# Full-row score products, forget sums stored by heads, two spill buffers and an early first weight in a two-layer streaming encoder

## The chip, the core and the metric

One core of a Trainium2 chip runs the whole program in one launch. Its engines work side by side: TensorE (PE: products, with its weight loads listed apart as PEld), VectorE (DVE), ScalarE (ACT), GpSimd (POOL) and SyncE (SP), which issues the DMA transfers. Each engine takes its instructions in the order in which they were laid down at build time; an instruction that waits holds up all that stand behind it on its engine. The metric is the device time of one execution in microseconds (us).

## The reference

Two layers work on 1024 prompt rows and 32 sample rows of width 1024. Each has an input projection, two branches with gates, an output projection and a LayerNorm.

```
# layer 0
a = causal_dwconv(a_val * sigmoid(a_glu)); a = silu(LN(a)) * silu(a_gate)
ck = cumsum(log_sigmoid(f_logit + b_f))                    # per head
s = (q @ k.T) * 64**-0.5 + cq[:, None] - ck[None, :]       # 8 heads x 64, causal
o = softmax(s) @ v * silu(b_gate)
x = LN(alpha * x + concat(a, o) @ w_out)
# layer 1
c = multi_scale_pool(c_val) @ w_grp * scale * silu(c_gate)
score = sum_h iw[h] * relu(iq[h] @ ik.T / 8)               # 4 index heads x 64
keep the 256 best keys of each row; q, k, iq, ik are rotated (rope)
o = softmax(q @ k_kept.T * 64**-0.5) @ v_kept * silu(d_gate)
x = LN(alpha * x + concat(c, o) @ w_out)
```

Inputs and outputs are float32.

## The kernel before

**Numbers.** A float32 value is held as two fp32r tiles, a rounded high part and the rest (`split`: ACT rounds, DVE or POOL subtracts). A projection is three products, high weight by high input, low by high, high by low, 24 products for a group of 256 or 288 columns (`proj_steps`, L207). The low part of a 64-wide head is folded into the same 128 rows: `put_k` (L263) builds `kA` (rows 0 to 63 high part of the even head, rows 64 to 127 its low part) and `kB` (the odd head the other way round); `put_q` (L271) builds `q1` (the rounded pair of heads) and `qA`, `qB`, which hold the rest of q on the rows of the high part of k, and the rounded q on the rows of its low part.

**Score products.** `qk_mm` (L278) makes one tile of scores in two products into the same bank: L280 multiplies the 64 rows of one head of `q1` with 64 rows of `kA` or `kB`, and L281 multiplies all 128 rows of `qA` or `qB` with all 128 of the key tile. It is called in the attention of both layers (`first` in `attend`, 96 tiles each) and in the index scores of layer 1 (`scores`, 40 tiles).

**Attention.** `attend` goes over four pairs of heads p. In each, eight units (i, e), 256 queries of one head, are worked in a fixed order (`UNITS`). `merge` lays three streams side by side: `first` of a unit (score products, DVE adds bias and takes the running minimum at L362, ACT makes the exponential at L365), `second` of the unit before (PE transposes the exponentials at L411, ACT and DVE split them into `pth` and `ptl`, PE multiplies with v at L386), and the projections of the next pair's q and k (`qk0`, `qk1`), or, in the last pair, pieces of the output projection (`early_out`, L557). In layer 0 the bias of a tile is made by POOL (L891, L893) from `ckb`, a DMA of the head's running forget sums to all partitions (`fox_bias`, L887). The sums lie in the DRAM tile `ckd` by blocks of 128 keys, heads inside, so that one head is eight pieces of 512 bytes for every partition. When both heads of a unit are done, `spill` (L318) splits the result into `sph` and `spl`, one buffer each, and sends both to DRAM (`cod`); `cat_tiles` reads them back for the output projection.

**Start.** The nine row tiles of x come in (L671), PE transposes each (L252), ACT and DVE split them. The first weight is fetched and cut (`fetch`, `cut`) when the first projection asks for it; `start_plan` names the columns and `want` and `ready` run ahead by two.

**Between.** Layer 1 first projects index keys and queries (690 to 712 us), then v with the index scores in between (712 to 780), then finds the 256th best score of each row by halving intervals on DVE and ACT while the pooled mixer and the gates are projected (780 to 960), then builds the masks while the first q and k are projected.

**What sets the order.** The code is written in the order above; a scheduler at build time then places every instruction on its engine's queue. Tiles come from pools with a given number of buffers for each tag; a write to a buffer waits until the last reader of its former content is done. Tiles with the same tag share their buffers.

Of the kernel before, what the change touches and what calls it, by code (L numbers as in the profile page):

```python
# [10 lines left out]
FT = mybir.dt.float32  # L11
# [21 lines left out]
def tile_encoder(ctx: ExitStack, tc, A, O):  # L33
# [57 lines left out]
    ckd = dp.tile([11, 8, 128], FT, name="ckd")  # L91
# [10 lines left out]
    def split(hi, lo, src, eng=dve, alone=False):  # L102
        if alone:
            dve.tensor_copy(hi, src)
        else:
            act.activation(hi, src, AF.Copy)  # L106
        eng.tensor_tensor(lo, src, hi.bitcast(FT), op=OP.subtract)  # L107

    def fetch(src, c0, n, k0=0, kn=8):
        raw = wp.tile([128, 1056], FT, name="wraw", tag="wraw", bufs=2)  # L110
# [6 lines left out]
    def cut(raw, n, kn, own=None):  # L117
        if own is None:
            hi = wp.tile([128, 1056], FR, name="whi", tag="whi", bufs=3)
            lo = wp.tile([128, 1056], FR, name="wlo", tag="wlo", bufs=3)  # L120
# [124 lines left out]
    def to_xt(src, rows, X, t):  # L245
        g, off, _ = TT[t]
        for hf in range(2):
            ps = ps_t()
            pv = ps.rearrange("p (a n) -> p a n", a=4)
            for a in range(4):  # L250
                k = hf * 4 + a
                pe.transpose(pv[:, a, :rows], src[:rows, k * 128:(k + 1) * 128], ident[:rows, :rows])  # L252
            split(X[0][g][:, hf * 4:hf * 4 + 4, off:off + rows], X[1][g][:, hf * 4:hf * 4 + 4, off:off + rows],
                  pv[:, :, :rows])
# [16 lines left out]
    def put_q(q1, qA, qB, r):  # L271
        act.activation(q1, r, AF.Copy)  # L272
        act.activation(qA[64:128], r[0:64], AF.Copy)
        act.activation(qB[0:64], r[64:128], AF.Copy)
        dve.tensor_tensor(qA[0:64], r[0:64], q1[0:64].bitcast(FT), op=OP.subtract)
        dve.tensor_tensor(qB[64:128], r[64:128], q1[64:128].bitcast(FT), op=OP.subtract)
# [67 lines left out]
    def attend(l, ap, qk, stacks, bias_fn, last, order, early):  # L344


        def first(p, i, e, stacks, bias, pt):
            kA, kB, qs = stacks
            q1, qA, qB = qs[i]
            k2, q2 = (kA, kB)[e], (qA, qB)[e]  # L350
            for j in range(2):
# [6 lines left out]
                for c in range(nch):  # L358
                    c0, cn = c * 512, min(512, n - c * 512)
                    ps = ps_s()  # L360
                    qk_mm(ps[:, :cn], e, q1, q2, j * 128, 128, k2, c0, cn)
# [8 lines left out]
        def second(p, i, e, pt, v2, cat):  # L370
# [9 lines left out]
            def pv(pth, ptl, blocks):  # L380
# [10 lines left out]
                ot = ap.tile([128, 256], FT, name="ot", tag="ot", bufs=1)  # L391
                act.activation(ot[hb:hb + 64], po[64:128, :256], AF.Copy)
                dve.tensor_tensor(op[hb:hb + 64], po[0:64, :256], ot[hb:hb + 64], op=OP.add)
                if e == 1:
# [4 lines left out]
                    else:  # L399
                        spill(ap, cod[l][i][p], op)  # L400
# [256 lines left out]
    ckt = ep.tile([128, 11, 8], FT, name="ckt")  # L657
# [9 lines left out]
    with tc.tile_pool(name="p1", bufs=1, reuse_waits="tile") as p1:  # L667
        for t, (g, off, rows) in enumerate(TT):
            xt = p1.tile([128, D], FT, name="xrow", tag="xrow", bufs=3)
            src = A["x_prompt"][0, t * 128:(t + 1) * 128] if t < 8 else A["x_sample"][0]  # L670
            sp.dma_start(xt[:rows], src)  # L671
            to_xt(xt, rows, X0, t)
# [22 lines left out]
        start_plan(w0, [(c0 + c * 128, 128) for c in range(4) for c0 in (512, 0)])  # L695
# [31 lines left out]
        def wload_vf(k0, own=None):  # L727
            raw = wp.tile([128, 1056], FT, name="wraw", tag="wraw", bufs=2)
# [40 lines left out]
    def qk0(p):  # L769
# [6 lines left out]
        def evac(g, ps, nm, scale):  # L776
            if g % 2 == 0:
                hold[nm] = pz.tile([128, 544], FT, name=nm, tag=nm, bufs=1)
            r = hold[nm]
            c0 = 256 * (g % 2)  # L780
# [11 lines left out]
        def ev_q(g, t0, n, ps):  # L792
            r = evac(g, ps, "qr", SC)
            q1, qA, qB = (pz.tile([128, 256], FR, name=nm, tag=nm, bufs=4) for nm in ("q1", "qA", "qB"))
            c0 = 256 * (g % 2)
            put_q(q1, qA, qB, r[:, c0:c0 + 256])
            qs[g] = q1, qA, qB
            if n > 256:
                dve.tensor_copy(qkS0[:, p, 0, :], r[:, 512:544])
# [4 lines left out]
    def forget_sums():  # L804
# [3 lines left out]
        act.activation(ckt.rearrange("p t h -> p (t h)"), pck, AF.Copy)  # L808
# [33 lines left out]
    with tc.high_priority():  # L842
        rstd = p1r.tile([128, 1086], FT, name="rstd")
        for g, (s0, n) in enumerate(((0, 256), (256, 256), (512, 256), (768, 318))):
# [3 lines left out]
            pvv = ps_s()[:, :n]  # L848
            for c in range(4):
# [98 lines left out]
    masks = lp.tile([128, sum(MW)], BF, name="masks")  # L948
# [55 lines left out]
    with tc.tile_pool(name="p4", bufs=1, reuse_waits="tile") as p4:  # L1004
# [38 lines left out]
        for p in range(2):  # L1043
            q1, qA, qB = (p4.tile([128, SEQ - 256], FR, name=f"{nm}{p}") for nm in ("qi1", "qiA", "qiB"))
            qi_st.append((q1, qA, qB))

            def ev_iq(g, t0, n, ps, p=p, q1=q1, qA=qA, qB=qB):
# [535 lines left out]
```

## Time and profile before

| what | value |
|---|---|
| time, median of 3 executions | 1373.24 us (1371.05 to 1373.4) |
| time of the profiled execution | 1373.61 us |
| its span, first to last instruction | 1371.9 us |
| mean granted TensorE clock | 0.962 of 2.4 GHz |
| PE busy | 1290.8 us (94%) |
| DVE busy | 994.8 us (73%) |
| ACT busy | 694.1 us (51%) |
| POOL busy | 244.5 us (18%) |

The profile is of one execution; 1.7 us of its time lie outside the span. A busy share is an average over stages with different limits. PE counts as busy as long as any product is under way, and products overlap, so a busy PE can still lose time between the starts of its products; starts are therefore read one against the next. The clock of TensorE is granted at one of two levels, 2.4 GHz (shown as 1.00) or 1.2 GHz (0.50).

### The profile page before, as it was taken

How to read it: one execution, taken by the hardware profiler on the slowest of the kernel's cores; microseconds unless marked ns; L12 is line 12 of the kernel's file. 1: busy time of each engine (PE TensorE's matmuls, PEld its weight loads, DVE VectorE, ACT ScalarE, POOL GpSimd, SP SyncE). 2: the span in 40 equal slices, each digit the busy share in tenths (PEclk: the TensorE clock that was granted, in tenths of full speed). 3: DMA queues.
4: the chain of work that ended last, by engine and by line, in shares of the span. 5: the costliest groups of instructions: out<-in, count | busy, mean ns of one | idle time of the engine just before them, and what ended most of it. 6: DMA issues, size and time to landing. Idle time of an engine off the chain costs nothing. (4 is left out here: it accounts for less than half of the span.)

```text
span 1371.9 us, 25230 instructions
## 1 busy us (share of the span) xinstructions
PE 1290.8 (94%) x9341; PEld 1176.9 (86%) x9344; DVE 994.8 (73%) x2227; ACT 694.1 (51%) x1484; POOL 244.5 (18%) x529
## 2 busy tenths in 40 slices
PE   7999999999899998999999978699999999989997
PEld 6999999987787886899997778598988888868997
DVE  4699997374666666647846599995677878776467
ACT  4111232494766665512256676587356767675210
POOL 0000060003333332100021245365011000100000
PEclk9999999997999998999999998899999999999999
DMA  6113312333222356353242212123333223562502
GB/s 207 47 48 88 117 47 75 108 125 90 80 74 68 73 155 192 109 169 108 92 129 64 80 48 80 31 80 94 96 79 98 58 75 87 156 203 67 199 35 93
DMA packets 175063, 134.63 MB, mean 98 GB/s; under 512 B 37242, under 2 KB 163666, under 8 KB 174940
## 3 DMA queue, kind: packets, MB, share of 16 engines
q1 hardware_dynamic: 174940, 133.02, 33.3%
q8 instruction: 73, 1.20, 0.4%
q14 instruction: 50, 0.41, 0.1%
HBM read 85.09 MB, written 42.48 MB: 93 GB/s over the span
## 5 line engine op out<-in xcount | busy, mean ns | idle before, releaser
L841 DVE SCALAR_TENSOR_TENSOR acc<-apad,vT,acc 128x1086 f32<-128x1086 f32 x120 | 156.2, 1338 | 1.1
L107 DVE TENSOR_TENSOR ptl<-bank,pth 128x512 fp32r<-128x512 f32 (+1 forms) x160 | 99.5, 633 | 49.9 <-ACT pth L106 49.0
L207 PE MATMUL bank<-x1h,whi 128*128 128x256 f32 (+3 forms) x848 | 130.0, 293 | 0.1
L207 PE MATMUL bank<-x1h,wlo 128*128 128x256 f32 (+3 forms) x848 | 128.2, 291 | 0.0
L207 PE MATMUL bank<-x1l,whi 128*128 128x256 f32 (+3 forms) x848 | 126.9, 290 | 0.0
L365 ACT ACTIVATE s<-s,mn 128x896 f32<-128x896 f32 (+7 forms) x128 | 98.9, 773 | 51.6 <-DVE mn L362 50.7
L207 PE MATMUL bank<-x0h,whi 128*128 128x256 f32 (+1 forms) x768 | 118.5, 296 | 4.3 <-ACT whi L106 3.2
L106 ACT ACTIVATE pth<-bank 128x512 fp32r<-128x512 f32 (+1 forms) x160 | 86.4, 550 | 69.3 <-PE bank L411 67.6
L207 PEld LDWEIGHTS bank<-x1h,whi 128*128 128x128 f32 (+1 forms) x848 | 116.7, 193 | 2.0 <-issue 0.7
L207 PEld LDWEIGHTS bank<-x1h,wlo 128*128 128x128 f32 (+1 forms) x848 | 116.2, 193 | 1.0 <-issue 0.4
L207 PE MATMUL bank<-x0h,wlo 128*128 128x256 f32 (+1 forms) x768 | 115.6, 292 | 0.0
L207 PEld LDWEIGHTS bank<-x1l,whi 128*128 128x128 f32 (+1 forms) x848 | 113.9, 190 | 1.3 <-issue 0.8
L207 PE MATMUL bank<-x0l,whi 128*128 128x256 f32 (+1 forms) x768 | 113.0, 287 | 0.0
L207 PEld LDWEIGHTS bank<-x0h,whi 128*128 128x128 f32 x768 | 106.2, 197 | 5.9 <-ACT whi L106 3.5
L207 PEld LDWEIGHTS bank<-x0h,wlo 128*128 128x128 f32 x768 | 105.1, 195 | 0.6
L1260 ACT ACTIVATE jka<-sc,neg 128x768 bf16<-128x768 f32 (+2 forms) x96 | 99.7, 1038 | 8.7 <-POOL neg L1287 3.9
L207 PEld LDWEIGHTS bank<-x0l,whi 128*128 128x128 f32 x768 | 102.1, 190 | 0.5
L107 DVE TENSOR_TENSOR wlo<-wraw,whi 128x1024 fp32r<-128x1024 f32 (+2 forms) x55 | 66.9, 1216 | 48.5 <-ACT whi L106 47.4
L411 PE MATMUL bank<-ident,s 128*128 128x128 f32 x576 | 96.2, 283 | 5.3 <-DVE ptl L107 3.0
L106 ACT ACTIVATE whi<-wraw 128x1024 fp32r<-128x1024 f32 (+2 forms) x62 | 64.9, 1049 | 63.1 <-PE bank L207 37.7
L386 PE MATMUL bank<-pth,v 128*128 128x256 f32 x320 | 93.2, 309 | 1.4 <-ACT pth L106 1.4
L386 PE MATMUL bank<-ptl,v 128*128 128x256 f32 x320 | 85.0, 296 | 0.5 <-DVE ptl L107 0.5
(410 smaller groups left out, 2733.2 us busy)
## 6 DMA issues: line engine op xcount, KB each, us to landing
wraw<-in_o_w_in_dram SPq DMA_DIRECT2D x26, 512.0 KB, 4.0
wraw<-in_e_w_in_dram SPq DMA_DIRECT2D x24, 512.0 KB, 4.2
xrow<-in_x_prompt_dram SPq DMA_DIRECT2D x8, 512.0 KB, 4.5
sgd<-sgc SPq DMA_DIRECT2D x32, 128.0 KB, 1.9
out_dram<-ko SPq DMA_DIRECT2D x16, 256.0 KB, 2.5
vf<-vd SPq DMA_DIRECT2D x16, 256.0 KB, 3.0
ckb<-ckd SPq DMA_DIRECT2D x8, 512.0 KB, 9.9
sg<-sgd SPq DMA_DIRECT2D x32, 128.0 KB, 2.5
```

The costliest lines, as they stand in the source:

```text
L106: act.activation(hi, src, AF.Copy)
L107: eng.tensor_tensor(lo, src, hi.bitcast(FT), op=OP.subtract)
L207: pe.matmul(ps, w[:, k, :], x[g][:, k, :], start=i == 0, stop=i == 23)
L365: act.activation(s[:, :n], s[:, :n], AF.Exp, bias=mn[:, c:c + 1], scale=-1.0, accum_out=grp[p, i][0][:, j, e:e + 1])
L386: pe.matmul(po[:, j0 * 128:j0 * 128 + w], v2[e][:, k, :], src[:, b0:b0 + w], start=k == 0 and x == 0, stop=k == 2 * i + 1 and x == 1)
L411: pe.transpose(ps[:, c:c + 128], pt[j][:, k * 128:(k + 1) * 128], ident)
L841: dve.scalar_tensor_tensor(ac, apad[c][:, j:j + 1086], vT[:, c, j:j + 1], ac, op0=OP.mult, op1=OP.add)
L1260: act.activation(jka[:, :n], sct[COL[ND + j]], AF.Sign, bias=neg[:, j:j + 1].bitcast(FT), accum_out=cnta[:, j:j + 1])
```

## The change

- **Score products.** `q1` becomes `qz`, a tile of two halves: in half 0 the rows of the even head hold q and the other 64 rows are zero, in half 1 the other way round. Both products of `qk_mm` then use all 128 rows, with the same sum. POOL writes the zeros (two memsets for each q tile), and ACT fills `qz` with two instructions of 64 rows where one of 128 rows filled `q1`.
- **Forget sums.** `ckd` is laid out by heads. One head is then 4096 bytes in a row for every partition in `ckb`. The transpose before it reads `ckh`, written by heads; the sample's reads follow.
- **Spill buffers.** In layer 0 `spl` has two buffers, and `sph` shares two buffers with `ot`. In layer 1 `sph` shares one buffer with `ot`, and `spl` one with `rx`.
- **Start.** The first two row tiles come in two halves each. The first weight is fetched right behind them and cut after the transposes of the second. Nine products on a zeroed tile stand ahead of the first transpose.
- **Room.** `kos` shares the buffer of `ko`; `wraw`, `whi`, `wlo`, `qr`, `rstd`, `trib`, `sg`, `eq` and `eqT` become smaller; the masks move to a pool that opens after the mixer.

The core of the diff:

```diff
-    ckd = dp.tile([11, 8, 128], FT, name="ckd")
+    ckd = dp.tile([8, 11, 128], FT, name="ckd")
...
+    def blank_q(pl, nm, n, **tag):
+
+        qz = pl.tile([128, 2, n], FR, name=nm, **tag)
+        pool.memset(qz[64:128, 0].bitcast(FT), 0.0)
+        pool.memset(qz[0:64, 1].bitcast(FT), 0.0)
+        return qz
+
-    def put_q(q1, qA, qB, r):
-        act.activation(q1, r, AF.Copy)
+    def put_q(qz, qA, qB, r):
+        act.activation(qz[0:64, 0], r[0:64], AF.Copy)
+        act.activation(qz[64:128, 1], r[64:128], AF.Copy)
...
-    def qk_mm(ps, e, q1, q2, c0, m, k2, k0, n):
-        b = 64 * e
-        pe.matmul(ps, q1[b:b + 64, c0:c0 + m], k2[b:b + 64, k0:k0 + n], start=True, stop=False)
+    def qk_mm(ps, e, qz, q2, c0, m, k2, k0, n):
+        pe.matmul(ps, qz[:, e, c0:c0 + m], k2[:, k0:k0 + n], start=True, stop=False)
         pe.matmul(ps, q2[:, c0:c0 + m], k2[:, k0:k0 + n], start=False, stop=True)
...
-            kos = pl.tile([DS, 128], FT, name="kos", tag="kos", bufs=1)
+            kos = pl.tile([DS, 128], FT, name="kos", tag="ko", bufs=1)
...
-    def spill(pl, dst, src, n=256):
-        h = pl.tile([128, 256], FR, name="sph", tag="sph", bufs=1)
-        lo = pl.tile([128, 256], FR, name="spl", tag="spl", bufs=1)
+    def spill(l, pl, dst, src, n=256):
+        h = pl.tile([128, 256], FR, name="sph", tag="ot", bufs=2 - l)
+        lo = pl.tile([128, 256], FR, name="spl", tag=("spl", "rx")[l], bufs=2 - l)
...
-                ot = ap.tile([128, 256], FT, name="ot", tag="ot", bufs=1)
+                ot = ap.tile([128, 256], FT, name="ot", tag="ot", bufs=2 - l)
...
+        still = wp.tile([128, 1040], FR, name="wlo", tag="wlo", bufs=3).bitcast(BF)[:, :512]
+        dve.memset(still, 0.0)
+        idle = ps_o()
+        for _ in range(9):
+            pe.matmul(idle, still[:, 0:128], still, start=True, stop=True)
+        start_plan(w0, [(c0 + c * 128, 128) for c in range(4) for c0 in (512, 0)])
...
-            sp.dma_start(xt[:rows], src)
-            to_xt(xt, rows, X0, t)
+            if t < 2:
+                for c0 in (0, 512):
+                    sp.dma_start(xt[:rows, c0:c0 + 512], src[:, c0:c0 + 512])
+            else:
+                sp.dma_start(xt[:rows], src)
+            if t == 1:
+                want(0)
+            up = to_xt(xt, rows, X0, t)
+            if t == 1:
+                with tc.issue_after(up.ins):
+                    ready(0)
...
-            sp.dma_start(ckb.rearrange("p (t q) -> p t q", q=128),
-                         bass.AP(tensor=ckd.tensor, offset=ckd.offset + h * 128, ap=[[0, 128], [1024, 8], [1, 128]]))
+            sp.dma_start(ckb, bass.AP(tensor=ckd.tensor, offset=ckd.offset + h * 1408, ap=[[0, 128], [1, SEQ]]))
```

The products themselves stay where they were on PE. Three queues show what moves. On SP, at the start of the program, before the change (`xrow` is a row tile of x, `wraw` a raw weight, the rest small vectors):

```order
L671 DMA xrow<-in_x_prompt_dram 128x1024 x3
L675 DMA vecs<-in_e_conv_w_dram 31x512
L677 DMA vecs<-in_e_conv_b_dram 1x512
L677 DMA vecs<-in_e_conv_ln_g_dram 1x512
L677 DMA vecs<-in_e_conv_ln_b_dram 1x512
L677 DMA vecs<-in_o_pool_scale_dram 1x512
L685 DMA cc<-in_cache_conv_dram 30x512
L112 DMA wraw<-in_e_w_in_dram 128x8x128
L671 DMA xrow<-in_x_prompt_dram 128x1024 x2
```

and with it:

```order
L689 DMA xrow<-in_x_prompt_dram 128x512 x4
L113 DMA wraw<-in_e_w_in_dram 128x8x128
L691 DMA xrow<-in_x_prompt_dram 128x1024
L700 DMA vecs<-in_e_conv_w_dram 31x512
L702 DMA vecs<-in_e_conv_b_dram 1x512
L702 DMA vecs<-in_e_conv_ln_g_dram 1x512
L691 DMA xrow<-in_x_prompt_dram 128x1024
```

The first weight moves from the tenth transfer to the fifth, ahead of the third row tile.

On ACT, in layer 0, where the keys of the next pair of heads go out (`ko` the prompt's, `kos` the sample's, `qr` the raw q), before:

```order
L376 ACTIVATE rx<-rc 128x256
L288 ACTIVATE ko<-bank_3827 128x512
L294 ACTIVATE kos<-bank_3835 32x128
L365 ACTIVATE s,rs<-s,mn 128x768
L781 ACTIVATE qr<-bank_3778 128x256
L272 ACTIVATE q_3859<-qr 128x256
L273 ACTIVATE qA<-qr 64x256
L274 ACTIVATE qB<-qr 64x256
L365 ACTIVATE s,rs<-s,mn 128x640
```

and with the change:

```order
L385 ACTIVATE rx<-rc 128x256
L297 ACTIVATE ko<-bank_3858 128x512
L374 ACTIVATE s,rs<-s,mn 128x768
L805 ACTIVATE qr<-bank_3809 128x256
L281 ACTIVATE qz<-qr 64x256
L282 ACTIVATE qz<-qr 64x256
L283 ACTIVATE qA<-qr 64x256
L284 ACTIVATE qB<-qr 64x256
L303 ACTIVATE kos<-bank_3866 32x128
L374 ACTIVATE s,rs<-s,mn 128x640
```

`kos`, which now needs the buffer that `ko`'s transfer reads, stands six instructions later, and there is one more instruction for each q tile.

On POOL, in layer 0, in the first pair of heads (`s` is the tile that receives bias and scores), before:

```order
L893 AFFINE_SELECT s<-s 128x128 x2
L107 TENSOR_TENSOR wlo<-wraw,whi 128x1024
L891 TENSOR_SCALAR s<-ckb,ncq 128x512
L891 TENSOR_SCALAR s<-ckb,ncq 128x384
L893 AFFINE_SELECT s<-s 128x128 x2
```

and with the change:

```order
L916 AFFINE_SELECT s<-s 128x128 x2
L107 TENSOR_TENSOR wlo<-wraw,whi 128x1024
L276 MEMSET qz 64x256
L277 MEMSET qz 64x256
L914 TENSOR_SCALAR s<-ckb,ncq 128x512
L914 TENSOR_SCALAR s<-ckb,ncq 128x384
L916 AFFINE_SELECT s<-s 128x128 x2
```

The two memsets of a q tile of the next pair stand ahead of biases of this pair. They need a buffer whose former q tile PE has read for the last time.

## Rows read from the trace of the kernel before

**Rows 1.** Busy time by stage: the stretch in us from the span's start, its length, then busy us (and instructions) of PE, PEld, DVE, ACT and POOL, the granted clock, the DMA share and GB/s. In order: the index scores, the interval search, the attention of layer 1, the second quarter of that attention, the attention of layer 0.

```profile
712.00:780.00 68.00, 68.00 (x391) 52.67 (x389) 38.53 (x70) 40.90 (x87) 9.38 (x28) 1.00 0.25 70
780.00:960.00 180.00, 148.25 (x1109) 145.09 (x1109) 160.30 (x596) 129.50 (x265) 95.30 (x290) 0.90 0.24 69
1028.00:1267.00 239.00, 230.97 (x1519) 194.00 (x1518) 186.69 (x461) 164.10 (x372) 16.05 (x12) 0.99 0.36 104
1060.00:1130.00 70.00, 69.35 (x455) 57.78 (x456) 57.61 (x140) 51.02 (x112) 5.30 (x4) 1.00 0.23 63
312.00:571.00 259.00, 242.09 (x1497) 202.25 (x1495) 164.09 (x416) 160.40 (x361) 82.16 (x134) 0.92 0.36 97
```

**Rows 2.** Instructions of PE and PEld in order of time in the index scores: start us, duration us, engine, line, operation, output<-inputs, rows*columns of the weights, shape of the moving operand, count; in brackets idle time of the engine before it.

```profile
741.41 0.49 PE L280 MATMUL bank<-kiB,qi 64*128 64x512 f32 x1
741.83 0.19 PEld L281 LDWEIGHTS bank<-kiB,qiB 128*128 128x128 f32 x1 [0.24 <-issue]
741.83 0.50 PE L281 MATMUL bank<-kiB,qiB 128*128 128x512 f32 x1
742.16 1.12 PE L207 MATMUL bank<-x1h,wlo 128*128 128x256 f32 x8
743.12 0.38 PE L1142 MATMUL bank<-ident,vr 128*128 128x128 f32 x2
...
743.97 1.10 PE L207 MATMUL bank<-x1l,whi 128*128 128x256 f32 x8
745.00 0.38 PE L280 MATMUL bank<-kiB,qi 64*128 64x256 f32 x1
745.31 0.39 PE L281 MATMUL bank<-kiB,qiB 128*128 128x256 f32 x1
745.53 1.10 PE L207 MATMUL bank<-x1h,whi 128*128 128x256 f32 x8
```

**Rows 3.** The same view of PE in the attention of layer 0, a score tile of 128 keys.

```profile
521.58 0.32 PE L280 MATMUL bank<-kA,q 64*128 64x128 f32 x1
521.84 0.33 PE L281 MATMUL bank<-kA,qA 128*128 128x128 f32 x1
522.00 0.30 PE L411 MATMUL bank<-ident,s 128*128 128x128 f32 x1
```

**Rows 4.** All instructions of line 280 on PE: count, durations in ns (min/median/max), first and last start, and how many there are of each shape. `kA` and `kB` are of the attention of both layers together, `kiA` and `kiB` of the index scores.

```profile
L280 PE MATMUL bank<-kA,q x96: 322/490/792, 309.1 to 1240.5; 64*128 64x512 f32 x48, 64*128 64x384 f32 x16, 64*128 64x128 f32 x16, 64*128 64x256 f32 x16
L280 PE MATMUL bank<-kB,q x96: 323/491/792, 328.6 to 1258.9; 64*128 64x512 f32 x48, 64*128 64x384 f32 x16, 64*128 64x128 f32 x16, 64*128 64x256 f32 x16
L280 PE MATMUL bank<-kiA,qi x20: 324/491/500, 712.4 to 773.1; 64*128 64x512 f32 x12, 64*128 64x384 f32 x4, 64*128 64x128 f32 x2, 64*128 64x256 f32 x2
L280 PE MATMUL bank<-kiB,qi x20: 323/491/502, 713.1 to 774.9; 64*128 64x512 f32 x12, 64*128 64x384 f32 x4, 64*128 64x128 f32 x2, 64*128 64x256 f32 x2
```

**Rows 5.** Instructions in order of time at the four places of layer 0's attention where PE stands still, with the instruction that ended the idle time.

```profile
319.48 2.10 POOL L891 TENSOR_SCALAR s<-ckb,ncq 128x896 f32<-128x896 f32 x2 [6.27 <-DMA ckb<-ckd]
321.27 0.49 PE L280 MATMUL bank<-kA,q 64*128 64x512 f32 x1 [3.00 <-DVE mn L362]
...
373.42 0.99 DVE L107 TENSOR_TENSOR spl<-op,sph 128x256 fp32r<-128x256 f32 x1 [5.25 <-DMA cod<-spl]
375.07 0.69 PE L422 MATMUL bank<-ident,rx 128*128 128x128 f32 x2 [3.92 <-DVE ptl L107]
...
442.29 0.69 PE L422 MATMUL bank<-ident,rx 128*128 128x128 f32 x2 [3.25 <-DVE ptl L107]
...
529.60 1.26 PE L557 MATMUL bank<-whi,cat0h 128*128 128x256 f32 x2 [3.66 <-DMA cat0h<-cod]
```

**Rows 6.** Busy time, with the columns of Rows 1, of the stretches behind the first three of these places.

```profile
322.00:340.00 18.00, 18.00 (x60) 13.16 (x59) 7.00 (x20) 6.86 (x15) 3.53 (x8) 0.53 0.26 64
373.00:381.00 8.00, 5.93 (x26) 5.30 (x27) 5.42 (x12) 3.64 (x9) 1.68 (x3) 0.57 0.26 77
441.00:449.00 8.00, 6.71 (x28) 5.97 (x28) 5.06 (x12) 3.63 (x9) 1.03 (x3) 0.57 0.66 65
```

**Rows 7.** DMA issues by tile: count, KB each, median us from issue to landing.

```profile
wraw<-in_e_w_in_dram SPq DMA_DIRECT2D x24, 512.0 KB, 4.2
ckb<-ckd SPq DMA_DIRECT2D x8, 512.0 KB, 9.9
out_dram<-r SPq DMA_DIRECT2D x8, 512.0 KB, 2.6
```

**Rows 8.** The start in order of time.

```profile
5.73 0.40 SPq L112 DMA_DIRECT2D wraw<-in_e_w_in_dram  x1
12.96 1.06 ACT L106 ACTIVATE whi<-wraw 128x1024 fp32r<-128x1024 f32 x1 [3.55 <-DMA wraw<-in_e_w_in_dram]
14.06 2.08 PE L207 MATMUL bank<-x0h,whi 128*128 128x256 f32 x8 [3.21 <-ACT whi L106]
```

**Rows 9.** The instruction that fills `q1` in layer 0 (durations in ns, min/median/max), and two lines of who waited for whom (us in total, times, longest us).

```profile
L272 ACT ACTIVATE q<-qr x16: 400/412/419, 303.8 to 516.4; 128x256 fp32r<-128x256 f32 x16
POOL s L891 <- PE bank L411: 135.5, 23, 14.9
DVE s L362 <- POOL s L891: 5.1, 1, 5.1
```

**Rows 10.** Landing of the transfers that read `sph`, in us from issue (24 transfers, min/median/max).

```profile
DMA to landing us min/median/max: 1.7/2.4/8.0
```

More of the change, by code (lines that the diff above doesn't have):

```diff
@@ L252, in to_xt @@
                 pe.transpose(pv[:, a, :rows], src[:rows, k * 128:(k + 1) * 128], ident[:rows, :rows])
-            split(X[0][g][:, hf * 4:hf * 4 + 4, off:off + rows], X[1][g][:, hf * 4:hf * 4 + 4, off:off + rows],
-                  pv[:, :, :rows])
+            up = split(X[0][g][:, hf * 4:hf * 4 + 4, off:off + rows], X[1][g][:, hf * 4:hf * 4 + 4, off:off + rows],
+                       pv[:, :, :rows])
+        return up
     def rows_out(pl, src_cols, n, dst):
@@ L399, in pv @@
                     else:
-                        spill(ap, cod[l][i][p], op)
+                        spill(l, ap, cod[l][i][p], op)
             for kk in range(0, 2 * i + 2, 2):
@@ L656, in tile_encoder @@
     qkS0 = ep.tile([128, 4, 2, DS], FT, name="qkS0")
-    ckt = ep.tile([128, 11, 8], FT, name="ckt")
+    ckh = ep.tile([128, 8, 11], FT, name="ckh")
     ncq = ep.tile([128, 11, 8], FT, name="ncq")
@@ L727, in wload_vf @@
         def wload_vf(k0, own=None):
-            raw = wp.tile([128, 1056], FT, name="wraw", tag="wraw", bufs=2)
+            raw = wp.tile([128, 1040], FT, name="wraw", tag="wraw", bufs=2)
             rv = raw[:, :1040].rearrange("p (k n) -> p k n", n=260)
@@ L793, in ev_q @@
             r = evac(g, ps, "qr", SC)
[L794 to L797, printed above, removed]
+            qA, qB = (pz.tile([128, 256], FR, name=nm, tag=nm, bufs=4) for nm in ("qA", "qB"))
+            qz = blank_q(pz, "qz", 256, tag="qz", bufs=4)
+            put_q(qz, qA, qB, r[:, 0:256])
+            qs[g] = qz, qA, qB
             if n > 256:
-                dve.tensor_copy(qkS0[:, p, 0, :], r[:, 512:544])
+                dve.tensor_copy(qkS0[:, p, 0, :], r[:, 256:288])
         yield from proj_steps(w0, 2048 + p * 128, 128, X0, ev_k)
@@ L848, in tile_encoder @@
             pvv = ps_s()[:, :n]
+            rstd = p1r.tile([128, 318], FT, name="rstd", tag="rstd", bufs=2)
             for c in range(4):
@@ L1043, in tile_encoder, with ev_iq @@
         for p in range(2):
-            q1, qA, qB = (p4.tile([128, SEQ - 256], FR, name=f"{nm}{p}") for nm in ("qi1", "qiA", "qiB"))
-            qi_st.append((q1, qA, qB))
-            def ev_iq(g, t0, n, ps, p=p, q1=q1, qA=qA, qB=qB):
+            qA, qB = (p4.tile([128, SEQ - 256], FR, name=f"{nm}{p}") for nm in ("qiA", "qiB"))
+            qz = blank_q(p4, f"qiz{p}", SEQ - 256)
+            qi_st.append((qz, qA, qB))
+            def ev_iq(g, t0, n, ps, p=p, qz=qz, qA=qA, qB=qB):
                 if g == 1:
@@ L1305, in masking @@
     def masking(p4):
-        trib = p4.tile([128, SEQ], BF, name="trib")
+        trib = p4.tile([128, 640], BF, name="trib")
         pool.memset(trib, 1.0)
@@ L1333, in s2 @@
             eq = held[i][1]
-            eqT = p4.tile([128, 8, 128], BF, name="eqT", tag="eqT", bufs=2)
+            eqT = p4.tile([128, nb, 128], BF, name="eqT", tag=f"eqT{i % 2}", bufs=1)
             held[i] += (eqT,)
@@ L1458, in tile_encoder @@
     mctx.close()
+    rctx = ExitStack()
+    pr = rctx.enter_context(tc.tile_pool(name="pr", bufs=1, reuse_waits="tile", side="right"))
+    masks = pr.tile([128, sum(MW)], BF, name="masks")
     qctx = ExitStack()
@@ L1484, in ev_q @@
             for j in range(2):
-                q1, qA, qB = (pq.tile([128, 256], FR, name=nm, tag=nm, bufs=4) for nm in ("q1", "qA", "qB"))
-                put_q(q1, qA, qB, r[:, 256 * j:256 * j + 256])
-                qs[g - 1 + j] = q1, qA, qB
+                qA, qB = (pq.tile([128, 256], FR, name=nm, tag=nm, bufs=4) for nm in ("qA", "qB"))
+                qz = blank_q(pq, "qz", 256, tag="qz", bufs=4)
+                put_q(qz, qA, qB, r[:, 256 * j:256 * j + 256])
+                qs[g - 1 + j] = qz, qA, qB
             if n > 256:
```

62 lines of the change are left out of this document (30 added, 32 removed).

## The prediction

> **What bounds the kernel now.** I read busy time by stage first [rows 1]. In the index scores and in the attention of both layers PE is busy nearly throughout (68.00 of 68.00 us, 242.09 of 259.00, 230.97 of 239.00), and DVE stands at 57%, 63% and 78%. In the interval search it is the other way round: DVE 160.30 of 180.00 (89%), PE with long gaps. So time taken from PE shows in the score and attention stages, and the search keeps its length and only begins earlier. PE's busy share hides gaps between starts, so next come the products one by one [rows 2, 3], then how many of each shape there are [rows 4], then the places where PE stands still [rows 5], the clock behind them [rows 6], the transfers that they wait for [rows 7] and the start [rows 8].
>
> **What one score tile costs.** The eight projection products from 742.16 to 743.12 take 0.12 us each with their weight loads, for 256 columns [rows 2]. A 512-column tile of scores takes 741.41 to 741.83 for L280 and on to 742.16 for L281: 0.42 and 0.33. PEld is idle 0.24 us before L281's load, and load and product are then recorded at the same moment: the 128-row load was not made ready behind the 64-row product. A third loss lies ahead of L280: the eight products from 743.97 are followed only at 745.00, 1.03 us where eight took 0.96, so 0.07. Together 0.82 us. A 256-column tile: 0.31 + 0.22 + 0.07 = 0.60. A 128-column tile [rows 3]: 0.26 + 0.16 + 0.07 = 0.49.
>
> If both products use all 128 rows, they should follow like projection products. For 256 columns that is 0.12 each, so 0.24 for a tile and 0.36 saved. For 128 columns I leave 0.12 each: 0.25 saved. For 512 columns no row shows two full-row products in succession; at the pitch of the 256 columns one costs at most 0.24, and at 2.4 GHz the columns alone need 0.21. I take 0.23, so 0.46 for a tile and 0.36 saved (0.34 to 0.40). For 384 columns, between, 0.36 as well.
>
> Counts [rows 4]: half of `kA` and `kB` is one layer, so 48 tiles of 512 and 16 each of 384, 256 and 128. One layer: 48 x 0.36 + 16 x (0.36 + 0.36 + 0.25) = 32.8 us of PE. Index scores: 24 x 0.36 + 8 x 0.36 + 4 x 0.36 + 4 x 0.25 = 14.0. In all 79.6 us of PE. What of it is time depends on the stage.
>
> [...]
>
> **Layer 0's attention.** Products: 32.8, of which I take 31. Afterwards DVE would be busy 164.09 and ACT 160.40 plus 16 x 0.41 = 167 [rows 1, 9] of some 209 us, 79% and 80%. In the second quarter of layer 1's attention DVE is at 82% and ACT at 73%, and PE is still busy 69.35 of 70 us [rows 1], so PE should stay the bound.
>
> Waits [rows 5]: at 318 PE stands 3.00 us, because POOL's first bias waits 6.27 us for `ckb`. At 371 DVE waits 5.25 us to write `spl`, whose transfer has not left, and PE stands 3.92; at 439 the same, 3.25. Together 10.2. The transfer of `ckb` takes 9.9 us to land where a weight of the same 512 KB, also in 512-byte pieces, takes 4.2, and 512 KB in 4096-byte rows going out 2.6 [rows 7]. In 4096-byte rows I take 4.2 for `ckb` (ends 2.6 and 9.9). That is 5.7 us earlier, more than the first wait; and at the other two places the second buffer of `spl` removes the cause even if `ckb` stays slow. I take 9 of the 10.2.
>
> Clock [rows 6]: behind these three places the granted clock is 0.53, 0.57 and 0.57, so 1.2 GHz most of the time, with PE busy 18.0, 5.93 and 6.71 us. At the full clock that work would take 8.5 + 2.5 + 2.9 = 13.9 us less. In each case PE stood still before the clock fell; without the standstill I expect the fall not to come there, and take 10 of the 13.9 (0 if it comes elsewhere). The fourth place, 3.66 us at 525.9 for the attention results read back [rows 5], I leave as it is: the second buffer helps those transfers leave, but less PE time covers them. Sum for layer 0: 31 + 9 + 10 = 50.
>
> **Index scores.** 14.0 of 68 us; then ACT stands at 40.90 plus some 2 for the four further fills of q, 77%, and DVE at 69% [rows 1]. I take 12.5.
>
> **Layer 1's attention.** 32.8 us of PE, but DVE has 186.69 us of work in 239 [rows 1]. The fullest DVE row of the trace is 89%. At that share the stage needs 186.69 / 0.89 = 210 us, 29 less. Its second quarter alone needs 57.61 / 0.89 = 64.7, 5.3 less, where products free 32.8 x 70 / 239 = 9.6; at that rate the stage gets 18. I take 23 (10 to 33): here DVE becomes the bound.
>
> **Start.** The first weight is issued at 5.73 us, ACT gets it at 12.96 after 3.55 of idling, and the first projection product starts at 14.06 [rows 8]. Now it is the fifth transfer, behind 1 MB instead of 1.5 MB. By the place in the queue it goes out some 3 us earlier and has a third less ahead of it. I take 4.5 us. Against it: nine products on zeros, 512 columns each, at 1.2 GHz 0.43 us each, 3.8 in all, stand ahead of the first transpose, and later row tiles come behind the weight. Ends: a loss of 1 and a gain of 7.
>
> **At nothing.** The further fill of a q tile is 0.41 us of ACT [rows 9], counted above. The memsets of `qz` run on POOL, busy 82.16 of 259.00 us [rows 1]; they wait for PE, and behind them in POOL's queue stand biases that DVE needs. POOL now waits 135.5 us for free `s` tiles and DVE has waited for such a bias once, 5.1 us [rows 9], so there is slack; if it is gone, each of the 12 memset pairs behind running products costs what it waits. The smaller tiles and the masks' new pool add no instruction. ACT's waits on shared buffers are the fifth case.
>
> **Sum.** 50 + 12.5 + 23 + 4.5 = 90 us off the profiled execution's own 1373.6: 1283.6. The median is 0.4 lower than that, which I neglect.
>
> **The cases.**
> 1. Forecast, 1284: the loads slip behind the products, layer 0 and the scores stay with PE, layer 1 goes over to DVE. Own range 1268 to 1305. Chance 0.59.
> 2. The other engines take over sooner, since every step of attention goes PE, DVE, ACT, PE with two banks of each kind: half of the products' gain in layer 0 (16.4), 0.6 in the scores (8.4), 0.3 in layer 1 (9.8), waits 9, clock 8, start 3. That is 54.6, 1319. For it: DVE and ACT near 80% with few buffers; against it: the quarter with DVE at 82% and PE full. Chance 0.17.
> 3. PE stays the bound everywhere: 32.8 + 10.2 + 13.9, 14.0, 32.8, start 7: 110.7, so 1263. Against it: DVE would have to be full in layer 1. Chance 0.13.
> 4. The change doesn't do what it says: full-row products still wait for their own loads, as L281 does now, 0.33, 0.22 and 0.16 us for 512, 256 and 128 columns. A tile is then 0.66, 0.44 or 0.32, some 0.16 saved, 232 x 0.16 = 37 in place of 79.6: 15.4 a layer, 6.4 in the scores, with waits 9, clock 10 and start 4.5 it makes 60.7, 1313. Against it: the projections [rows 2]. Chance 0.05.
> 5. Slower: ACT's queue. 40 instructions of ACT now write a buffer that a transfer reads (24 `ot`, 8 `rx`, 8 `kos`, counted in the program), where 21 `sph` did. Behind each stand exponentials and copies for which PE and DVE wait. The transfers of `sph` land 1.7 to 8.0 us after issue, median 2.4 [rows 10]. From 90 / 40 = 2.25 us for each the gain is gone; with 2.4 it is 96, 1380. Against it: several instructions of ACT lie between most such pairs. Chance 0.04.
>
> The remaining 0.02 is no change. A measurement of this kernel can tell about 0.2% from none. Faster is cases 1 to 4, 0.94; the same 0.02; slower 0.04. The range goes from below case 3 (its products at 0.40 give 6 less: 1257) to above case 2: 1257 to 1322; it leaves out the fifth case and the ends of the second.
>
> **What would show it.** The first products of score tiles with 128 rows and, for 512 columns, 0.21 to 0.24 us from start to start of both; PEld without idle time ahead of them. Index scores in 55 to 57 us, layer 0's attention in 205 to 215, layer 1's in 210 to 222 with DVE near 89%. `ckb` landing in 3 to 5 us, no wait of DVE for `cod`, clock 1.00 through the first half of layer 0's attention. First projection product at 9 to 10 us. Wrong would be: starts still 0.3 apart (case 4), PE idle in layer 0 behind DVE or ACT (case 2), ACT idle ahead of `ot` or `kos` until a transfer lands (case 5).

## The result and the profile after

Before 1373.18 us (median of 4 runs, 1371.05 to 1373.4), after 1310.05 us (4 runs, 1308.19 to 1312.58): ratio 0.9545, 95% interval 0.9526 to 0.9564. The gain is 63 us where 90 were forecast. The time lies in the whole range of 1257 to 1322, but outside the 1268 to 1305 of the case that was forecast. The profiled execution after has a span of 1308.1 us.

First the stretches, each from the first to the last start of the first product of a score tile (L280 before, L289 after), as the two traces give them in us:

| stretch | before | after | gained | forecast |
|---|---|---|---|---|
| start to layer 0's first score tile | 309.1 | 302.4 | 6.7 | 4.5 |
| layer 0's attention | 258.4 | 222.7 | 35.7 | 50 |
| from there to the index scores | 144.9 | 145.7 | -0.8 | 0 |
| index scores | 62.5 | 54.1 | 8.4 | 12.5 |
| interval search and what lies around it | 249.9 | 248.5 | 1.4 | 0 |
| layer 1's attention | 234.2 | 222.9 | 11.3 | 23 |
| the rest | 113.0 | 111.7 | 1.3 | 0 |

All three stages with products gave less than forecast. Did the products fail to shrink? Instructions of PE in order of time in the index scores after (columns as in [rows 2]):

```profile
702.05 0.28 PE L289 MATMUL bank<-kiB,qiz 128*128 128x256 f32 x1
702.18 0.28 PE L290 MATMUL bank<-kiB,qiB 128*128 128x256 f32 x1
702.30 1.11 PE L208 MATMUL bank<-x1h,whi 128*128 128x256 f32 x8
...
705.85 0.39 PE L289 MATMUL bank<-kiA,qiz 128*128 128x512 f32 x1
706.08 0.40 PE L290 MATMUL bank<-kiA,qiA 128*128 128x512 f32 x1
706.32 0.39 PE L289 MATMUL bank<-kiB,qiz 128*128 128x512 f32 x1
```

They did not: from start to start a 512-column tile takes 706.32 - 705.85 = 0.47 us (before 0.82 [rows 2], forecast 0.46), a 256-column tile behind projection products 702.30 - 702.05 = 0.25 (0.60, 0.24). So the freed time was given back elsewhere. Busy time by stage after, columns as in [rows 1]: layer 0's attention, layer 1's attention, index scores.

```profile
302.60:525.40 222.80, 200.24 (x1489) 185.79 (x1488) 164.33 (x409) 165.98 (x376) 92.61 (x158) 0.98 0.38 114
...
973.50:1196.60 223.10, 202.85 (x1481) 184.25 (x1480) 180.11 (x452) 167.20 (x380) 26.22 (x37) 0.99 0.38 110
...
671.00:725.20 54.20, 51.18 (x358) 46.82 (x357) 37.20 (x68) 36.72 (x84) 7.86 (x22) 1.00 0.30 83
```

Before, over the same stretches of the two attentions (layer 0's first):

```profile
309.50:568.00 258.50, 241.59 (x1489) 201.59 (x1488) 162.61 (x409) 161.15 (x363) 83.34 (x134) 0.92 0.37 99
...
1025.00:1259.30 234.30, 226.56 (x1480) 189.74 (x1479) 184.33 (x452) 161.45 (x364) 17.40 (x13) 0.99 0.36 105
```

PE stands still for 22.6, 20.3 and 3.0 us; before it was 16.9, 7.7 and, in the scores, 0 [rows 1]. The forecast had wanted less idle time in layer 0 and DVE at 89% in layer 1. DVE has 81% there, PE 91%.

The largest piece is one place, three times in layer 0 and once in layer 1. ACT in order of time; then SP's queue; then PE:

```profile
337.31 0.41 ACT L284 ACTIVATE qB<-qr 64x256 fp32r<-64x256 f32 x1
341.37 0.27 ACT L303 ACTIVATE kos<-bank 32x128 f32<-32x128 f32 x1 [3.65 <-DMA out_dram<-ko]
...
336.37 0.37 SPq L113 DMA_DIRECT2D wraw<-in_e_w_in_dram  x1
336.80 0.57 SPq L298 DMA_DIRECT2D out_dram<-ko  x1
...
341.69 1.12 PE L420 MATMUL bank<-ident,s 128*128 128x128 f32 x4 [3.95 <-ACT kos L303]
```

This is the prediction's own sign of its fifth case. `kos` now uses the buffer of `ko`, so ACT may write it only when the transfer that reads `ko` has landed. ACT wrote `ko` from 334.00 to 334.58, SP issued the transfer at 336.80 (a weight whose buffer was still in use stood ahead of it in the queue), and it took 4.6 us to land. Behind `kos` in ACT's queue stood an exponential and the copies on which PE and DVE depend. Then the clock fell; columns as in [rows 1]:

```profile
340.30:347.10 6.80, 5.41 (x24) 5.23 (x25) 2.74 (x6) 3.56 (x8) 0.00 (x0) 0.50 0.07 20
```

The granted clock is 0.50 throughout. A score product of 256 columns takes 0.22 us there from start to start (346.66 to 346.88); above, at 1.00, it takes 0.13 (702.05 to 702.18). Who waited for whom (us in total, times, longest), PE in layer 0's attention, then in layer 1's:

```profile
PE bank L420 <- ACT kos L303: 7.9, 3, 4.0
PE bank L289 <- DVE mn L371: 5.5, 8, 1.7
PE bank L420 <- DVE ptl L107: 4.6, 4, 1.5
...
PE bank L289 <- DVE mn L371: 4.2, 4, 2.3
PE bank L395 <- ACT pth L106: 2.7, 5, 1.1
PE bank L420 <- DVE ptl L107: 2.3, 5, 0.9
...
PE bank L420 <- ACT kos L303: 2.0, 1, 2.0
```

In layer 0 `kos` leads, and no wait for the attention results read back is left (3.66 us before [rows 5], which the forecast had left as it was); in layer 1 the wait is spread over a dozen kinds. Of the transfers, `ckb` (columns as in [rows 7]) came out as forecast:

```profile
ckb<-ckd SPq DMA_DIRECT2D x8, 512.0 KB, 4.5
```

The start, beside [rows 8]: the first weight is issued and the first projection product starts at

```profile
2.66 0.43 SPq L113 DMA_DIRECT2D wraw<-in_e_w_in_dram  x1
...
11.02 1.19 PE L208 MATMUL bank<-x0h,whi 128*128 128x256 f32 x8
```

which is 3.0 us earlier than before, 1.5 less than forecast.

### The profile page after: what moved, and what is told of

The parts are those of the page before. It is cut to its first block, busy times and chain, and to the rows that moved or that the text cites. A ratio compares the mean times of both kernels' runs of the same rounds, so it can differ in the third digit from the quotient of the medians.

```text
span 1308.1 us, 25434 instructions
## 1 busy us (share of the span) xinstructions
PE 1208.9 (92%) x9353; PEld 1146.7 (88%) x9353; DVE 991.4 (76%) x2228; ACT 705.6 (54%) x1520; POOL 269.8 (21%) x597
## 5 line engine op out<-in xcount | busy, mean ns | idle before, releaser
L374 ACT ACTIVATE s<-s,mn 128x896 f32<-128x896 f32 (+7 forms) x128 | 98.9, 773 | 28.2 <-DVE mn L371 26.9
L208 PE MATMUL bank<-x0h,whi 128*128 128x256 f32 (+1 forms) x768 | 112.9, 287 | 1.0 <-ACT kr L805 1.0
L106 ACT ACTIVATE pth<-bank 128x512 fp32r<-128x512 f32 (+1 forms) x160 | 85.8, 549 | 32.8 <-PE bank L420 31.7
L208 PEld LDWEIGHTS bank<-x0h,whi 128*128 128x128 f32 x768 | 100.8, 189 | 2.8 <-ACT kr L805 1.3
L395 PE MATMUL bank<-pth,v 128*128 128x256 f32 (+1 forms) x320 | 93.2, 308 | 4.8 <-ACT pth L106 4.7
L420 PEld LDWEIGHTS bank<-ident,s 128*128 128x128 f32 x576 | 67.1, 142 | 33.5 <-ACT kos L303 11.0
```

Source lines behind the costliest of these rows:

```text
L106: up = act.activation(hi, src, AF.Copy)
L208: pe.matmul(ps, w[:, k, :], x[g][:, k, :], start=i == 0, stop=i == 23)
L374: act.activation(s[:, :n], s[:, :n], AF.Exp, bias=mn[:, c:c + 1], scale=-1.0, accum_out=grp[p, i][0][:, j, e:e + 1])
L395: pe.matmul(po[:, j0 * 128:j0 * 128 + w], v2[e][:, k, :], src[:, b0:b0 + w], start=k == 0 and x == 0, stop=k == 2 * i + 1 and x == 1)
L420: pe.transpose(ps[:, c:c + 128], pt[j][:, k * 128:(k + 1) * 128], ident)
```

## Experiments

**Theory**: the products gave what they should. In layer 0 the change adds one new wait, ACT's for `ko`'s transfer, and the clock behind it. In layer 1 the freed time turned into waits of PE for the step before, with no engine at its limit. **Rivals**: DVE bounds layer 1, as forecast; or the gain is mostly from the waits and the clock. Each edit lets the planner set the order anew, so a few instructions change places beside the edit.

**A buffer of its own for `kos`.**

```diff
-            kos = pl.tile([DS, 128], FT, name="kos", tag="ko", bufs=1)
+            kos = pl.tile([DS, 128], FT, name="kos", tag="kos", bufs=1)
...
-        cks = p1r.tile([88, 128], FT, name="cks")
+        cks = p1r.tile([88, 128], FT, name="cks", tag="sq", bufs=2)
...
-                rc = ap.tile([128, 2, 2], FT, name="rc", tag="rc", bufs=2)
+                rc = ap.tile([128, 2, 2], FT, name="rc", tag="rc", bufs=2 - l)
```

> The changed kernel with a buffer of its own for kos again (room for it comes from cks, which shares a tile of sq, and in layer 1 from one rc buffer fewer). Theory: ACT's wait in front of kos for the transfer that reads ko is passed on to PE, and the clock falls behind it. Then the stops of 3.95, 3.36, 0.6 and 2.0 us ahead of L420 go, some 9.9 us, and with them up to 5.1 us of the 10.2 us at half clock that follow two of them: 1295 to 1300. Rival: attention is a chain of PE, DVE and ACT in which freed time is taken up by the next wait, as it was in layer 1: at most 3 us, 1307 to 1310.

Measured 1298.55 us, ratio 0.9472 (0.9444 to 0.9501), clear of the changed kernel's interval. Layer 0's attention, and the place of the first stop, in the view of [rows 1]; then ACT there:

```profile
304.20:514.10 209.90, 195.72 (x1489) 181.73 (x1488) 161.22 (x408) 164.43 (x375) 93.12 (x158) 1.00 0.39 121
...
339.00:347.00 8.00, 8.00 (x66) 7.72 (x65) 6.59 (x21) 6.59 (x16) 2.88 (x6) 1.00 0.66 198
...
335.70 0.58 ACT L297 ACTIVATE ko<-bank 128x512 f32<-128x512 f32 x1
336.17 0.25 ACT L303 ACTIVATE kos<-bank 32x128 f32<-32x128 f32 x1
```

Layer 0 falls from 222.7 to 209.9, 12.8 less: 8.4 us less idle time of PE, of which 7.9 is the wait for `kos`, and 4.5 us less busy time, with the clock at 1.00 in the whole stage. Against before that is 48.5 us, and 50 were forecast. PE still stands still for 14.2 us, 2.7 less than before. The longest waits are of the kind that leads in layer 1:

```profile
PE bank L289 <- DVE mn L371: 5.1, 8, 1.7
PE bank L420 <- DVE ptl L107: 4.4, 4, 1.3
```

Layer 1 stays (223.7): there the wait was 2.0.

**The first product on 64 rows again.**

```diff
-        pe.matmul(ps, qz[:, e, c0:c0 + m], k2[:, k0:k0 + n], start=True, stop=False)
+        b = 64 * e
+        pe.matmul(ps, qz[b:b + 64, e, c0:c0 + m], k2[b:b + 64, k0:k0 + n], start=True, stop=False)
```

> The changed kernel with the first product of each score tile on 64 rows again (the same qz, one half of it); all else as changed. By the step on products, as forecast: 31 + 12.5 + 23 = 66.5 us slower, 1376. By what the two traces show (81 us of PE's time between starts went, 37 us of other waits came, up to 10 of them from kos): 45 to 55 us slower, 1355 to 1365. Rival: most of the gain is from the waits and the clock: under 25 us slower, below 1335.

Measured 1349.87 us, ratio 0.9847 (0.9813 to 0.9881). So the full rows are worth 40 us of the 63, below the 45 to 55 worked out from the traces and far below 66. The same stages (layer 0, scores, layer 1):

```profile
303.60:539.60 236.00, 228.36 (x1489) 191.50 (x1488) 163.22 (x410) 166.68 (x378) 90.81 (x158) 0.99 0.36 108
683.80:747.80 64.00, 63.65 (x358) 48.50 (x357) 37.16 (x68) 38.43 (x83) 7.28 (x22) 1.00 0.26 71
996.20:1240.00 243.80, 235.25 (x1481) 195.46 (x1480) 184.47 (x453) 168.35 (x382) 25.51 (x37) 0.95 0.35 101
```

PE's wait for `kos` in layer 0, in this run:

```profile
PE bank L421 <- ACT kos L304: 4.8, 2, 2.8
```

With narrow products PE is idle 7.6 (4.8 of it for `kos`), 0.4 and 8.6 us: it was the bound. Full rows take 28.1, 12.5 and 32.4 us off its busy time and put 14.9, 2.7 and 11.7 us of idle time in. The wait for `kos` grows from 4.8 to 7.9 us, so it is 3.1 of the 14.9; the rest is new waiting in the chain, in layer 0 as in layer 1. Layer 1's difference of 20.7 us also holds a lower clock here, 0.95. Layer 0 with narrow products is 22.4 us shorter than before, with 4.8 us of `kos` in it: that is what the waits and the clock are worth without the full rows, where 9 and 10 were forecast.

**One buffer of `spl` in layer 0.**

```diff
-        lo = pl.tile([128, 256], FR, name="spl", tag=("spl", "rx")[l], bufs=2 - l)
+        lo = pl.tile([128, 256], FR, name="spl", tag=("spl", "rx")[l], bufs=1)
```

> The changed kernel with one buffer of spl in layer 0 in place of two. As forecast: DVE waits again for the transfer of the tile before at two places, PE stands 3 to 4 us at each and the clock falls behind: 7 to 13 us slower, 1317 to 1323. Rival: with ckb landing in 4.5 us and not in 9.8, the transfers of spl leave in time anyway, and one buffer would have done: 1308 to 1312.

Measured 1310.25 us, ratio 0.9562 (0.9532 to 0.9592): no change. What DVE waits for ahead of `spl`, in the whole program (us, times):

```profile
  DMA cod<-spl: 0.4, 1
```

The second buffer buys nothing once `ckb` is fast.

**The forget sums by tiles again**, both the storing and the reads of `ckb` and `cb` as before; the core of it:

```diff
-            sp.dma_start(ckb, bass.AP(tensor=ckd.tensor, offset=ckd.offset + h * 1408, ap=[[0, 128], [1, SEQ]]))
+            sp.dma_start(ckb.rearrange("p (t q) -> p t q", q=128),
+                         bass.AP(tensor=ckd.tensor, offset=ckd.offset + h * 128, ap=[[0, 128], [1024, 8], [1, 128]]))
```

> The changed kernel with the forget sums stored by tiles again, so that ckb is read in pieces of 512 bytes. As forecast: ckb lands in some 10 us, POOL's first bias comes late, PE stands 3 us near the start of layer 0's attention and the clock falls behind for up to 17 us: 6 to 11 us slower, 1316 to 1321. Rival: the transfers are hidden behind work but for the first: 3 us, 1313, the clock unmoved.

Measured 1323.6 us, ratio 0.9646 (0.9615 to 0.9678): 13.5 us slower, more than expected. Landing of `ckb` (min/median/max), and PE's waits in layer 0:

```profile
DMA to landing us min/median/max: 8.8/9.9/13.4
...
PE bank L289 <- DVE mn L371: 8.5, 8, 3.6
PE bank L420 <- ACT kos L303: 7.9, 3, 3.8
PE bank L566 <- DMA cat0h<-cod: 5.2, 1, 5.2
```

Layer 0 takes 234.1 us, 11.4 more. Besides the first stop (3.6) the read-back of the attention results at the stage's end comes 5.2 us late, and the clock of the stage is 0.96, not 0.98. The spill does not wait here, with two buffers. So DVE's waits for `cod` of [rows 5] stay away with fast `ckb` and one buffer of `spl`, and with slow `ckb` and two; only fast `ckb` shows in the time.

**The start**: without the nine products on zeros, and with the first weight behind all row tiles.

```diff
-        for _ in range(9):
-            pe.matmul(idle, still[:, 0:128], still, start=True, stop=True)
...
-            if t == 1:
-                want(0)
-            up = to_xt(xt, rows, X0, t)
-            if t == 1:
-                with tc.issue_after(up.ins):
-                    ready(0)
+            to_xt(xt, rows, X0, t)
```

> The changed kernel without the nine products on zeros at the start. If they are what holds the clock up through the first row tiles and products (granted clock 1.00 from 11 to 97 us, before 0.97 from 14 to 100): 2 to 4 us slower, 1312 to 1314. If they only stand ahead of the first transposes: 0 to 1 us faster, 1309 to 1310.

> The changed kernel with the first weight fetched and split behind all nine row tiles again; the halved row transfers and the nine products on zeros stay. As forecast the early weight is worth the 3.0 us by which the first projection product came earlier: 1313. Rival: the projections stand behind the row tiles and their splits anyway (ACT and DVE work on them until some 20 us), and it is worth under 1 us: 1310 to 1311.

Measured 1310.55 us (ratio 0.9547, 0.952 to 0.9573) and 1313.06 (0.9565, 0.9537 to 0.9592). Neither is separated from the changed kernel. In the profiles the first projection product starts at 12.40 and 15.20 us, not 11.02, and layer 0's first score tile comes at 305.3 and 305.6 us, not 302.4. But in the ten other runs below and above, whose start is that of the changed kernel, it comes at 302.4 to 304.5. So both parts point to a gain of some 1 to 3 us each, and neither is shown in the time.

**One more small instruction per step in layer 1**, on one engine at a time, 80 times on DVE, 80 on ACT, 160 on PE:

```diff
+                if l == 1:
+                    dve.tensor_tensor(ptl[:, :128], ps[:, :128], pth[:, :128].bitcast(FT), op=OP.subtract)
...
+                if l == 1:
+                    act.activation(pth[:, :128], ps[:, :128], AF.Copy)
...
+                if l == 1:
+                    for _ in range(2):
+                        pe.transpose(ps[:, :128], pt[0][:, kk * 128:(kk + 1) * 128], ident)
```

> The changed kernel; in layer 1's attention each of the 80 subtractions that make ptl is followed by one more of its first 128 columns (the same values again), some 0.2 us of DVE each, 16 to 20 us in all. If DVE bounds that stage, as forecast: 15 to 20 us slower. If the stage is a chain of PE, ACT and DVE in which no engine is full: a third to two thirds of it, 5 to 13 us. If PE bounds it: under 3 us.

> The changed kernel; in layer 1's attention each of the 80 copies that make pth is preceded by one of its first 128 columns (the same values), some 0.25 us of ACT each, 20 us in all. If DVE or PE bounds that stage: under 3 us slower. If the stage is a chain of PE, ACT and DVE: a third to two thirds, 6 to 14 us.

> The changed kernel; in layer 1's attention each of the 80 groups of transposes is followed by two more of its first block (the same values again), some 0.12 us of PE each, 19 us in all. If PE bounds that stage: 17 to 20 us slower. If it is a chain of PE, ACT and DVE: a third to two thirds, 6 to 13 us. If DVE bounds it, as forecast: under 3 us.

Measured 1312.61 us (ratio 0.9584, 0.9565 to 0.9604), 1313.2 (0.9583, 0.9564 to 0.9601) and 1325.15 (0.9666, 0.9643 to 0.969). Layer 1's attention in the three:

```profile
971.30:1197.00 225.70, 204.24 (x1481) 185.12 (x1480) 195.65 (x528) 166.83 (x380) 24.65 (x37) 0.98 0.37 109
...
972.60:1199.50 226.90, 205.53 (x1482) 183.72 (x1480) 183.70 (x452) 181.15 (x456) 25.30 (x37) 0.99 0.38 108
...
970.80:1208.40 237.60, 218.01 (x1635) 200.09 (x1634) 182.56 (x452) 167.65 (x380) 26.63 (x37) 0.99 0.36 103
```

Beside the row of the changed kernel: 15.5 us more of DVE lengthen the stage by 2.6 us, 14.0 of ACT by 3.8, 15.2 of PE by 14.5. In the four runs above that leave layer 1 alone (one buffer of `spl`, forget sums by tiles, both of the start) the stage takes 221.0 to 226.0 us, so the first two are hardly more than its own scatter; in the whole times, by their ratios, DVE and ACT cost some 5 us each, PE 17. PE still sets the pace in layer 1, although it stands idle 20 us of it. That rules out DVE as the bound, and also the theory's "a third to two thirds" for every engine: PE's work counts nearly in full, that of DVE and ACT for about a third at most.

**POOL's subtraction in four pieces**, on top of the buffer for `kos`; and **on DVE instead of POOL**.

```diff
-        eng.tensor_tensor(lo, src, hi.bitcast(FT), op=OP.subtract)
+        w = 256 if eng is pool else hi.shape[-1]
+        for c in range(0, hi.shape[-1], w):
+            eng.tensor_tensor(lo[..., c:c + w], src[..., c:c + w], hi[..., c:c + w].bitcast(FT), op=OP.subtract)
...
-        low[0] = pool
+        low[0] = dve
```

> The kernel with its own buffer for kos, and POOL's subtraction of a weight's low half cut into four of 256 columns each. Theory: DVE's 128x256 subtraction of spl, 0.42 us elsewhere, took 2.42 us at two places because POOL's 2.40 us subtraction of wlo held the same access to the tiles; cut in four, POOL lets it in between, and the two stops of PE of 1.7 us that follow shrink to under 0.7: 2 to 3 us faster than with kos alone, 1295.5 to 1296.5. Rival: POOL's four take longer in all (each with its own fixed cost), DVE waits as long, no change: 1298 to 1300.

> The kernel with its own buffer for kos, and the low halves of layer 0's weights during attention made by DVE and not POOL: six more instructions of 1.22 us on DVE, 7.3 us, and none of 2.40 on POOL. Theory of a chain in which each engine's time counts in part: the two stretched instructions (4.0 us) and their stops go, 7.3 us of DVE come, of which a third to a half shows: within 2 us of the kernel with kos alone, 1297 to 1301. If DVE had no part in what sets the time: 3 us faster, 1295.5. If DVE were the bound in layer 0: 3 to 7 us slower, 1302 to 1306.

Measured 1297.95 us (ratio 0.9455, 0.9427 to 0.9484) and 1300.22 (0.9481, 0.945 to 0.9513): neither separated from `kos` alone. DVE and POOL in the changed kernel, then in the one with four pieces:

```profile
365.07 2.42 DVE L107 TENSOR_TENSOR spl<-op,sph 128x256 fp32r<-128x256 f32 x1 [0.62 <-ACT sph L106]
...
364.82 2.40 POOL L107 TENSOR_TENSOR wlo<-wraw,whi 128x1024 fp32r<-128x1024 f32 x1 [1.48 <-ACT whi L106]
```

```profile
360.99 3.36 POOL L109 TENSOR_TENSOR wlo<-wraw,whi 128x256 fp32r<-128x256 f32 x4 [1.48 <-ACT whi L106]
...
361.25 0.77 DVE L109 TENSOR_TENSOR spl<-op,sph 128x256 fp32r<-128x256 f32 x1 [0.62 <-ACT sph L106]
```

The stretched subtraction shrinks from 2.42 to 0.77 us as expected, but layer 0's stage only from 209.9 to 209.3: PE's waits for `mn` fall from 5.1 to 3.3 us (the longest from 1.7 to 0.9), and its waits for the exponentials (L374, here L376) grow from 1.9 to 2.8. With the subtraction on DVE the stage takes 211.2, for some 7 us more work of DVE.

**A third bank for score tiles in layer 1**, taken from the attention sums, on top of the four pieces.

```diff
-    roles.update(ATT)
+    roles.update(dict(ATT, s=(2, 3, 6), o=(7,)))
```

> The kernel with its own buffer for kos and POOL's subtraction in four, and in layer 1's attention three banks for score tiles and one for the attention sums, in place of two and two. Theory: with the products shorter PE comes to a score tile's bank before DVE has read the tile before last out of it, and that is the largest share (11.5 of 32 us) of the time that PE stands in layer 1; a third bank takes 5 to 8 us of it, and with one bank for the sums PE waits 2 to 5 us more at the ends of units: 1291 to 1298. Rival: PE's order puts so much between that the bank is free and it is the tile's own data that are late: nothing gained, and 5 to 20 us lost at the ends of the 32 units: 1303 to 1318.

Measured 1297.4 us, ratio 0.9467 (0.945 to 0.9484): no change. PE's waits in layer 1, without and with the third bank (L291 is the first product, L397 the attention sums, L422 the transposes):

```profile
PE bank L291 <- DVE mn L373: 5.7, 6, 2.3
PE bank L397 <- ACT pth L106: 2.5, 7, 0.6
PE bank L291 <- ACT qz L283: 2.3, 2, 1.4
...
PE bank L422 <- DVE ptl L109: 1.2, 4, 0.3
```

```profile
PE bank L291 <- ACT qz L283: 4.9, 3, 3.4
PE bank L422 <- DVE ptl L109: 4.2, 9, 0.8
PE bank L291 <- DVE mn L373: 3.8, 4, 2.1
PE bank L397 <- DVE op L404: 3.7, 5, 1.2
```

The wait for DVE at the score tiles gets smaller, from 5.7 to 3.8 us, but the same product waits longer for `qz` (4.9, not 2.3), and the waits come back at the transposes and the sums.

## Why the prediction was right in sign and 26 us too hopeful

- **The time**: that it lies in the range does not make the forecast case right. 1310 us is next to the fourth case (1313) and the second (1319). The fourth did not happen at all; of the second the losses came, but not their reason, that the other engines take over; and one mechanism of the fifth came at four places. The products are the forecast's. That these add up to a time in the range is in part luck.
- **One score tile**: right, 0.47 and 0.25 us where 0.46 and 0.24 stood. The fourth case would have left 0.66 and 0.44. Full-row products, each with a weight load of its own, follow at 0.23 us for 512 columns and at 0.12 for 256 (705.85 to 706.08, 702.18 to 702.30). For the 0.21 that 512 columns alone were put at, the trace before has 0.22 (bf16 products of L1360 from 1021.82 to 1022.69 us, clock 1.00).
- **Layer 0, 50**: measured 35.7, and 48.5 with `kos` in its own buffer. The missing 13 are the fifth case's mechanism at three of its forty places. Without it the sum comes out, but not its terms: PE's busy time falls by 45.9 us (241.59 to 195.72), where products and clock were put at 31 + 10, and its idle time by 2.7, where 9 were forecast. The named waits went, and others of the chain came in their place; that the two errors cancel is luck. The step that failed is the sentence that several instructions lie between most such pairs: it was not asked for the pair in which two writes of one buffer stand close together. That no new wait comes was assumed, not looked up.
- **Waits and clock**: the waits for `cod` are gone and `ckb` lands in 4.5 us (forecast 4.2). The reason given for two of the three waits, the second buffer of `spl`, holds with slow `ckb`; with fast `ckb` one buffer is enough. The first half of layer 0 was not at 1.00, because of `kos`; without it the whole stage is.
- **Index scores, 12.5**: 8.4, which is the second case's 8.4. PE was busy throughout; now its busy time is 11.3 us less, and it stands 3.0 us that it did not.
- **Layer 1, 23**: 11.3, near the second case's 9.8. The step that failed is "here DVE becomes the bound" at 89%: DVE stands at 81%, and 15.5 us more work on it cost 2.6 us of the stage. PE's busy time did fall, from 226.56 to 202.85 us over the same stretch, but 12.5 us came back as idle time. The fall is 23.7 us where the count of products says 32.8; no run shows where the other 9 lie. The 89% came from another stage, the interval search, and did not carry over to this chain.
- **Start, 4.5**: 3.0 at the first product, within the ends. The nine products on zeros start 0.43 us apart (1.65 to 4.64), as forecast. The further 3.7 us up to layer 0 came little by little along the projections; some 2 us of that stretch differ between runs with the same start.
- **At nothing**: in layer 0 DVE waits 0.2 us for a bias of POOL, so the memsets of `qz` are hidden there. Before, it had waited not once, as the prediction says, but four times, 5.1 us for L891 and 2.7 us for L893. In layer 1 DVE waits 3.4 us, four times, for the rotary step on POOL, which shares its queue with them, and waited for none before. What that costs was not tested.

Open: what sets PE's idle time in layer 1. The amount of work on DVE and ACT has little part in it, and a third bank for score tiles only moves it; whether another order of PE's instructions would take it away was not tried.

## What to carry over

When two tiles share a buffer, list every pair of writes to it with the transfer that reads the first, its place in the queue and its landing time; three such pairs cost 13 us here, and a buffer of its own for the small tile, 512 bytes a partition, took it back. When the engine that sets the pace gets faster in a chain of three engines, count on a fifth to a half of its freed time coming back as waits, as in these three stages (14.9 of 28.1, 2.7 of 12.5 and 11.7 of 32.4 us). To learn which engine still sets the pace, add a little work to each in turn: that answered in three runs what the busy shares had answered wrongly. Compare the answer with how far the stage varies in runs that leave it alone.

## Not expected of the hardware

A DVE subtraction of 128x256 values, 0.42 us elsewhere, took 2.42 us beside a POOL subtraction of 2.40 us that had begun 0.25 us earlier, and 0.77 us beside one of 256 columns. DVE's subtraction ends 0.27 us after POOL's (367.49 and 367.22). That the two need the same access to the tiles is the author's explanation; the traces show these times alone.

A 256 KB transfer of `ko` took 4.6 us to land at the place shown above and 2.3 us at its quickest; with `ckb` in 512-byte pieces, the same 512 KB took 9.9 us at the median and not 4.5.
